# Outer products of a decoder step's sample states as 32-row products, one batch per quadrant of the array

## The chip, the cores and the metric

The kernel runs on one core of one Trainium2 chip. A core has TensorE (matrix products; the profile calls it PE, and its weight loads PEld), VectorE (DVE), ScalarE (ACT), GpSimd (POOL) and SyncE (SP), which issues DMAs. Each engine works through its own queue in order and waits on semaphores for the others. TensorE multiplies a stationary operand (the weights, rows x columns) with a moving one; the rows of both are partitions of the on-chip memory, and the result lands in PSUM. The time is device microseconds of a whole execution; less is better.

## The reference, cut to what matters

One decoder layer for a prompt of 256 tokens and for 8 sample sequences of 8 tokens each, all with d_model 2048 and shared weights: an mLSTM branch (4 heads of 256 x 256 state) and a GLA branch (4 heads of 128 x 256 state) in parallel, merged by gates, then a gated convolutional feed-forward. The samples come with states, one per batch and head, and each is updated with the outer products of that batch's own 8 keys and values:

```python
# mLSTM, per batch b and head h
C_new = decay[..., None, None] * C + jnp.einsum('bhl,blhd,blhe->bhde', w_end, kc, vc)
# GLA, per batch b and head h
S_new = (jnp.exp(b_end)[..., None] * S
         + jnp.einsum('bshd,bshe->bhde', kc * jnp.exp(b_end[:, None] - b), vc))
```

Within a chunk, the outputs also need products of a masked matrix A of token against token (64 x 64 for the samples) with the values. All data is fp32.

## The kernel before, in words

All 320 tokens (256 of the prompt, 64 of the samples) are the moving columns of the weight products. A product with fp32 weights and fp32 activations is made of three products in a faster format with rounded operands (`mm3`, L74 to L76): each operand is split into a rounded part (hi, made by ScalarE, L69 for weights) and the rest (lo, made by VectorE, L70). The results of weight products go to PSUM tiles called `big`, all others to tiles called `mx` (four banks of each kind) and `mxi`.

The stages follow one another: input and norm, then for each head h = 0..3 a GLA head (`gla_head`) and an mLSTM head (`mlstm_head`) with their projections, then the remaining gates, the output projection, and the feed-forward. Which instruction stands where in an engine's queue is decided by a scheduler that simulates the engines when the kernel is built; it interleaves the small work of the heads with the weight products of later projections. In the profiled execution the outer products lie between 146 and 465 us.

The samples' small products use a stack: the 64 sample tokens make two groups g of 32 tokens (4 batches of 8), and a group's 32 tokens stand four times above one another in 128 partitions, in the four quadrants r of 32 rows. In the keys' stack `ks` the quadrants hold hi, lo, hi, lo (`stacked`); in the values' stack `vs` they hold hi, hi, lo, lo (`values`). One product over 128 rows then sums all four combinations of parts, for all four batches of the group at once. To get the outer product of one batch alone, the keys are first multiplied by a mask: `km` holds copies of `ks` in which all rows of other batches are zero (`bm`, one column per batch), and each batch gets its products of 128 rows from `km` and `vs` (L687 in GLA, one per batch; L780 in mLSTM, two per batch). VectorE then adds the result to the decayed state (L691, L783), and a DMA on POOL's queue writes it out.

`sample_values` multiplies A of the samples with the values in the same stacked form: A's two 32 x 32 diagonal blocks are written into the quadrants of `asp` by ScalarE (L494) and VectorE (L496), and two products of 128 rows with `vs` (L498) are added to the result `mxi`, which `inter` began: products of a state with 32 columns of queries per batch, each in its own quadrant of columns (L572).

Further places at which an operand has fewer than 128 rows: transposes of short inputs (64 rows of x, L155; 32 rows of the normaliser state, L317; 64 rows of convolution state, L897) and the spreading of the norm factors (`lh`, L177, fp32, its last product with 64 rows). A product of plain fp32 operands is shown as two passes.

Of the kernel before, what the change touches and what calls it, by code (L numbers as in the profile page):

```python
# [10 lines left out]
F32 = mybir.dt.float32  # L11
# [6 lines left out]
P = 128  # L18
# [25 lines left out]
def step_kernel(ctx: ExitStack, tc: tile.TileContext, a: dict):  # L44
# [190 lines left out]
    with tc.tile_pool(name="mc", bufs=1, reuse_waits="tile") as mc, \  # L235
# [17 lines left out]
        for c0 in (0, 256):  # L253
# [11 lines left out]
        i16 = mc.tile([P, 16], F32, name="i16")  # L265
        nc.gpsimd.memset(i16, 1.0)
        nc.gpsimd.affine_select(i16, i16, pattern=[[-S, 16]], compare_op=ALU.is_ge, fill=0.0, base=0,
                                channel_multiplier=1)
        nc.gpsimd.affine_select(i16, i16, pattern=[[S, 16]], compare_op=ALU.is_ge, fill=0.0, base=S - 1,
                                channel_multiplier=-1)  # L270
        nc.gpsimd.tensor_tensor(i16[:, 0:8], i16[:, 0:8], i16[:, 8:16], op=ALU.add)
        bm = mc.tile([P, 4], F32, name="bm")
        nc.gpsimd.tensor_tensor(bm, i16[:, 0:4], i16[:, 4:8], op=ALU.add)
# [153 lines left out]
        asp = mc.tile([P, 2, P], F32R, name="asp")  # L427
        nc.gpsimd.memset(asp.bitcast(F32), 0.0)

        vH, vL, vs = (mc.tile([P, 2, 264], F32R, name=t)[:, :, 0:258] for t in ("vH", "vL", "vs"))  # L430
        for t, one in ((vH, 1.0), (vL, 0.0), (vs[0:64], 1.0), (vs[64:128], 0.0)):
            nc.gpsimd.memset(t[:, :, 256:258].bitcast(F32), one)

# [17 lines left out]
        def quads(name):  # L451
            t = w320(name)[:, 0:256]
            return t, t.rearrange("p (g r x) -> p g r x", g=2, r=4)

        def tok4(t):

            return t.rearrange("p (g x) -> p g x", g=2).unsqueeze(2).broadcast_to([P, 2, 4, 32])
# [9 lines left out]
        def values(v):  # L467

            pb = mx("mx8")
            for m in range(2):  # L470
                vr, vr4 = quads("vr")
                nc.gpsimd.tensor_copy(vr4, tok4(v[:, m, T:]))
                for g in range(2):
                    nc.tensor.transpose(pb[:, g * 256 + m * P:g * 256 + (m + 1) * P], vr[:, g * P:(g + 1) * P], ident)
            pa = natural(v)
            pav = pa.rearrange("p (j e) -> p j e", j=2)
            nc.scalar.activation(vH[:, :, 0:256], pav, AF.Copy)
            nc.vector.tensor_tensor(vL[:, :, 0:256], pav, vH[:, :, 0:256].bitcast(F32), op=ALU.subtract)
            pbv = pb.rearrange("p (g e) -> p g e", g=2)
            nc.scalar.activation(vs[:, :, 0:256], pbv, AF.Copy)  # L480
            nc.vector.tensor_tensor(vs[64:128, :, 0:256], pbv[64:128], vs[64:128, :, 0:256].bitcast(F32), op=ALU.subtract)
            return vH, vL

        def sample_values(pi, A, w):


            for g in range(2):
                Ag = A[32 * g:32 * g + 32, 32 * g:32 * g + 32].rearrange("p (q t) -> p q t", t=S)

                def quad(r):  # L490
                    return asp[32 * r:32 * r + 32, g].rearrange("p (q y) -> p q y", q=4)[:, :, 8 * g:8 * g + 8]

                for r in (g, g + 2):
                    nc.scalar.activation(quad(r), Ag, AF.Copy)  # L494
                for r in (1 - g, 3 - g):
                    nc.vector.tensor_tensor(quad(r), Ag, quad(g).bitcast(F32), op=ALU.subtract)  # L496
            for g in range(2):
                nc.tensor.matmul(pi[:, 0:w], asp[:, g], vs[:, g, 0:w], start=False, stop=(g == 1))  # L498
# [55 lines left out]
        def stacked(src, w):  # L554
            ks = wk.tile([P, 512], F32R, tag="ks", name="ks", bufs=1)
            nc.scalar.activation(ks[:, 0:w], src, AF.Copy)
            for r in (32, 96):
                nc.vector.tensor_tensor(ks[r:r + 32, 0:w], src[r:r + 32], ks[r:r + 32, 0:w].bitcast(F32), op=ALU.subtract)
            return ks[:, 0:w].bitcast(F32)
# [17 lines left out]
        def gla_head(h, q, k, v):  # L577
# [101 lines left out]
            for b0 in range(0, B, 4):  # L679
                km = wk.tile([P, 512], F32R, tag="km", name="km")  # L680
                kmv = km.rearrange("p (b d) -> p b d", b=4)
                nc.vector.tensor_tensor(kmv, ks[:, 32 * b0:32 * b0 + P].unsqueeze(1).broadcast_to([P, 4, P]),
                                        bm.unsqueeze(2).broadcast_to([P, 4, P]), op=ALU.mult)
                for i in range(0, 4, 2):
                    pS = mx("mx16")
                    for ii in range(2):
                        nc.tensor.matmul(pS[:, ii * 256:(ii + 1) * 256], kmv[:, i + ii], vs[:, b0 // 4, 0:256],  # L687
                                         start=True, stop=True)
                    for ii in range(2):
                        bb = b0 + i + ii  # L690
                        nc.vector.scalar_tensor_tensor(st0[:, bb], st0[:, bb], ebe[:, bb:bb + 1],  # L691
                                                       pS[:, ii * 256:(ii + 1) * 256], op0=ALU.mult, op1=ALU.add)
# [3 lines left out]
        def mlstm_head(h, q, k, v):  # L696
# [40 lines left out]
            for d in range(2):  # L737
                kr, kr4 = quads("kr")
                nc.vector.tensor_tensor(kr4, tok4(k[:, d, T:]), tok4(bc[:, N + 72:N + 136]), op=ALU.mult)
                for g in range(2):  # L740
                    nc.tensor.transpose(pk[:, g * 256 + d * P:g * 256 + (d + 1) * P], kr[:, g * P:(g + 1) * P], ident)
                ksum = wk.tile([P, B], F32, tag="ksum", name="ksum")
                nc.vector.tensor_reduce(ksum.rearrange("p (g b) -> p g b", g=2),
                                        kr4[:, :, 0].rearrange("p g (b t) -> p g b t", t=S),
                                        axis=mybir.AxisListType.X, op=ALU.add)
                nc.vector.tensor_tensor(n1[:, d], n1[:, d], ksum, op=ALU.add)
# [23 lines left out]
            for b0 in range(0, B, 2):  # L770
                km = wk.tile([P, 512], F32R, tag="km", name="km")
                kmv = km.rearrange("p (b d) -> p b d", b=2)
                nc.vector.tensor_tensor(kmv,
                                        ks[:, 256 * (b0 // 4):256 * (b0 // 4) + 256].unsqueeze(1).broadcast_to([P, 2, DH]),
                                        bm[:, b0 % 4:b0 % 4 + 2].unsqueeze(2).broadcast_to([P, 2, DH]), op=ALU.mult)
                for i in range(2):
                    bb = b0 + i
                    pC = mx("mx24")
                    for d in range(2):
                        nc.tensor.matmul(pC[:, d * 256:(d + 1) * 256], kmv[:, i, d * P:(d + 1) * P],  # L780
                                         vs[:, b0 // 4, 0:256], start=True, stop=True)
                    cf = c0t[bb // 4][:, bb % 4, :, 0:DH]
                    nc.vector.scalar_tensor_tensor(cf, cf, dec[:, bb:bb + 1], pC.rearrange("p (c e) -> p c e", c=2),  # L783
# [245 lines left out]
```

## Time and profile before

| what | value |
|---|---|
| time, median of 3 runs | 1915.32 us (1915.15 to 1915.62) |
| the profiled execution's own time | 1914.34 us |
| its span, first to last instruction | 1912.6 us |
| mean granted TensorE clock | 0.996 |
| TensorE products, busy | 1895.9 us (99%), 13123 records |
| VectorE / ScalarE / POOL busy | 1083.9 / 772.8 / 339.3 us |
| outer products in the trace | 32 in GLA (L687), 64 in mLSTM (L780) |

Rows of the profile give line, engine, operation, `out<-in` by the program's names, the weights' rows*columns for a product, the shape, and how many. In a timeline the first number is the start in us from the span's start, the second how long the row lasts from its first start to its last end. The durations of products overlap: each shows some 0.3 us from its start to the end of its results, while the next one starts long before; a product's share of TensorE's time is read from start to start. In tables by stretch, the columns behind the stretch are its length, busy time and count of each engine, the granted clock, the DMA share and GB/s.

### The profile page before, as it was taken

How to read it: one execution, taken by the hardware profiler on the slowest of the kernel's cores; microseconds unless marked ns; L12 is line 12 of the kernel's file. 1: busy time of each engine (PE TensorE's matmuls, PEld its weight loads, DVE VectorE, ACT ScalarE, POOL GpSimd, SP SyncE). 2: the span in 40 equal slices, each digit the busy share in tenths (PEclk: the TensorE clock that was granted, in tenths of full speed). 3: DMA queues.
4: the chain of work that ended last, by engine and by line, in shares of the span. 5: the costliest groups of instructions: out<-in, count | busy, mean ns of one | idle time of the engine just before them, and what ended most of it. 6: DMA issues, size and time to landing. Idle time of an engine off the chain costs nothing.

```text
span 1912.6 us, 32511 instructions
## 1 busy us (share of the span) xinstructions
PE 1895.9 (99%) x13123; PEld 1879.4 (98%) x13123; DVE 1083.9 (57%) x1666; ACT 772.8 (40%) x1096; POOL 339.3 (18%) x614
## 2 busy tenths in 40 slices
PE   9999999999999999999999999999999999999997
PEld 8999999999999999999999999999999999999997
DVE  5768686877544444446555545545554554555455
ACT  5544443454433333333344333433433443343345
POOL 4334241522000000021112102101110210111014
PEclk9999999999999999999999999999999999999998
DMA  8656676756555555565454444444445444444442
GB/s 250 201 140 195 189 220 184 226 171 216 168 146 152 148 150 153 146 189 167 151 151 146 152 153 146 154 146 152 150 148 155 144 154 148 150 153 146 154 148 93
DMA packets 300192, 311.03 MB, mean 163 GB/s; under 512 B 15268, under 2 KB 292026, under 8 KB 300041
## 3 DMA queue, kind: packets, MB, share of 16 engines
q1 hardware_dynamic: 287849, 283.53, 49.0%
q0 software_dynamic: 7296, 23.90, 3.6%
q8 instruction: 103, 1.69, 0.4%
q10 hardware_dynamic: 4896, 1.52, 0.3%
q14 instruction: 48, 0.39, 0.1%
HBM read 286.44 MB, written 22.47 MB: 162 GB/s over the span
## 4 chain that ended last, share of the span: by engine, by line


## 5 line engine op out<-in xcount | busy, mean ns | idle before, releaser
L70 DVE TENSOR_TENSOR wl<-raw,wh 128x1024 fp32r<-128x1024 f32 x504 | 628.6, 1247 | 608.9 <-ACT wh L69 608.4
L69 ACT ACTIVATE wh<-raw 128x1024 fp32r<-128x1024 f32 x504 | 534.4, 1060 | 881.0 <-PE big L75 735.4
L74 PE MATMUL big<-hH,wh 128*128 128x320 f32 x2832 | 878.6, 310 | 0.9 <-ACT wh L69 0.9
L75 PE MATMUL big<-hL,wh 128*128 128x320 f32 x2832 | 879.3, 311 | 0.0
L76 PE MATMUL big<-hH,wl 128*128 128x320 f32 x2832 | 877.5, 310 | 0.0
L74 PEld LDWEIGHTS big<-hH,wh 128*128 128x128 f32 x2832 | 532.3, 188 | 2.6 <-issue 1.2
L75 PEld LDWEIGHTS big<-hL,wh 128*128 128x128 f32 x2832 | 532.4, 188 | 1.0 <-issue 0.4
L76 PEld LDWEIGHTS big<-hH,wl 128*128 128x128 f32 x2832 | 532.3, 188 | 0.6
L75 PE MATMUL big<-aL,wh 128*128 128x320 f32 x704 | 217.9, 310 | 0.0
L76 PE MATMUL big<-aH,wl 128*128 128x320 f32 x704 | 217.6, 309 | 0.0
L74 PE MATMUL big<-aH,wh 128*128 128x320 f32 x704 | 215.8, 309 | 0.0
L76 PEld LDWEIGHTS big<-aH,wl 128*128 128x128 f32 x704 | 132.4, 188 | 0.0
L75 PEld LDWEIGHTS big<-aL,wh 128*128 128x128 f32 x704 | 132.4, 188 | 0.0
L74 PEld LDWEIGHTS big<-aH,wh 128*128 128x128 f32 x704 | 131.8, 188 | 0.0
L924 POOL COPY conv<-u 128x2 f32<-128x2 f32 x44 | 8.3, 188 | 527.4 <-DVE u L921 527.4
L855 POOL TENSOR_TENSOR g<-g 128x320 f32<-128x320 f32 x16 | 14.8, 925 | 366.4 <-DVE g L851 366.4
L75 PE MATMUL big<-mL,wh 128*128 128x320 f32 x256 | 78.8, 309 | 0.0
L74 PE MATMUL big<-mH,wh 128*128 128x320 f32 x256 | 78.7, 309 | 0.0
L76 PE MATMUL big<-mH,wl 128*128 128x320 f32 x256 | 78.7, 309 | 0.0
L962 DVE TENSOR_TENSOR x<-big,x 128x320 f32<-128x320 f32 x96 | 46.6, 488 | 46.5 <-PE big L76 46.5
L936 POOL TENSOR_TENSOR g<-g,uc 128x256 f32<-128x256 f32 x44 | 32.6, 742 | 211.9 <-DVE g L935 211.9
L75 PE MATMUL big<-yL,wh 128*128 128x320 f32 x192 | 59.2, 308 | 0.0
(394 smaller groups left out, 1790.7 us busy)
## 6 DMA issues: line engine op xcount, KB each, us to landing
raw<-in_w_in SPq DMA_DIRECT2D x176, 512.0 KB, 3.9
raw<-in_ffn_w_up SPq DMA_DIRECT2D x88, 512.0 KB, 3.5
raw<-in_ffn_w_gate SPq DMA_DIRECT2D x88, 512.0 KB, 3.7
raw<-in_ffn_w_down SPq DMA_DIRECT2D x88, 512.0 KB, 3.5
raw<-in_w_out SPq DMA_DIRECT2D x32, 512.0 KB, 3.5
C<-in_state_mlstm_C SPq DMA_DIRECT2D x32, 256.0 KB, 5.7
o_C_s<-C POOLq DMA_DIRECT2D x32, 256.0 KB, 4.0
raw<-in_w_branch_a SPq DMA_DIRECT2D x16, 512.0 KB, 3.4
```

Of the source, the lines that this page charges most:

```text
L69: nc.scalar.activation(hi, raw, AF.Copy)
L70: nc.vector.tensor_tensor(lo, raw, hi.bitcast(F32), op=ALU.subtract)
L74: nc.tensor.matmul(out, wh, xh, start=first, stop=False)
L75: nc.tensor.matmul(out, wh, xl, start=False, stop=False)
L76: nc.tensor.matmul(out, wl, xh, start=False, stop=last)
L855: nc.gpsimd.tensor_tensor(sg[m], sg[m], acc[m], op=ALU.add)
L924: nc.gpsimd.tensor_copy(conv1[:, 0:2, c], u[:, T:T + 2])
L936: nc.gpsimd.tensor_tensor(g[:, 0:T], g[:, 0:T], gel[m][:, 0:T], op=ALU.mult)
L962: nc.vector.tensor_tensor(x2[k], pt[:, :N], x2[k], op=ALU.add)
```

## The change

1. The stacks are laid out anew: quadrant r of group g now belongs to one batch, 4g + r, and holds that batch's 8 tokens four times, as the four parts (`quads`, `tok4`). A part's sign is in a table `sel` with a value for each partition, and one helper, `stack`, makes a whole stack in two instructions of 128 rows: ScalarE writes the rounded operand times +1 or -1, VectorE adds the operand times 0 or 1. Before, ScalarE wrote all rows and VectorE subtracted on 64 or twice 32 of them.
2. The outer product of a batch takes the 32 rows of its own quadrant of `ks` and `vs`. The masked copies `km` and the mask `bm` are gone. Each product in GLA has a PSUM bank to itself (`mx16`, half used), and two batches are issued together; in mLSTM, too, two batches have a bank each (`mx24`).
3. `sample_values` needs A's blocks spread over the quadrants in the new layout: two new fp32 products per head (L501) with a constant matrix `put` of 64 rows spread them, and `stack` writes the result into `asp`, twice a head.
4. The set-up of `bm` on POOL is replaced by ten small instructions on VectorE that make `part`, `sel` and `put`.

The PE queue in the first mLSTM head, at the outer products. Names: `km` and `ks` as above, `hH`, `hL` the parts of the activations, `wh`, `wl` those of the weights. Before:

```order
L76 MATMUL big<-hH_105,wl 128x320
L780 MATMUL mx_1811<-vs,km 128x256 x2
L74 MATMUL big<-hH_106,wh 128x320
L75 MATMUL big<-hL_122,wh 128x320
L780 MATMUL mx_1816<-vs,km 128x256 x2
L780 MATMUL mx_1823<-vs,km 128x256 x2
L76 MATMUL big<-hH_106,wl 128x320
L780 MATMUL mx_1828<-vs,km 128x256 x2
```

With the change, the same place. Both products of one PSUM tile (one batch) take the same 32 rows; the next tile takes the next quadrant:

```order
L76 MATMUL big<-hH_118,wl 128x320
L774 MATMUL mx_1810<-vs,ks 128x256 x2
L74 MATMUL big<-hH_115,wh 128x320
L75 MATMUL big<-hL_131,wh 128x320
L774 MATMUL mx_1811<-vs,ks 128x256 x2
L774 MATMUL mx_1820<-vs,ks 128x256 x2
L76 MATMUL big<-hH_115,wl 128x320
L774 MATMUL mx_1821<-vs,ks 128x256 x2
```

The products stand as close to weight products as before; the batches that follow are spread further, with two or three weight products between pairs. In the whole queue the 96 outer products stand in 31 runs between other work before, and in 50 with the change.

The PE queue in the first GLA head, at its outer products. Before, two batches share a tile:

```order
L74 MATMUL big<-hH_112,wh 128x320
L687 MATMUL mx_1206<-vs,km 128x256 x2
L687 MATMUL mx_1211<-vs,km 128x256 x2
L75 MATMUL big<-hL_128,wh 128x320
L687 MATMUL mx_1218<-vs,km 128x256 x2
L76 MATMUL big<-hH_112,wl 128x320
```

With the change; behind these three stand five more, each alone between weight products:

```order
L76 MATMUL big<-hH_113,wl 128x320
L689 MATMUL mx_1207<-vs,ks 128x256
L689 MATMUL mx_1208<-vs,ks 128x256
L689 MATMUL mx_1213<-vs,ks 128x256
L74 MATMUL big<-hH_114,wh 128x320
L75 MATMUL big<-hL_130,wh 128x320
```

The eight products of a GLA head stood in three runs, and now stand in six.

The PE queue where the first GLA head's new spreading products stand, with the numerator products (L518) behind them; the sample product L505 that needs their result comes after another 16 weight products:

```order
L76 MATMUL big<-hH_104,wl 128x320
L501 MATMUL mx_1123<-AT,put 128x32 x2
L518 MATMUL mx_1136<-vH,AH 128x256
L518 MATMUL mx_1136<-vL,AH 128x256
L518 MATMUL mx_1136<-vH,AL 128x256
```

L501 is new work in the queue; before, A went to `asp` by ScalarE and VectorE alone.

The diff, cut to its core:

```diff
-        i16 = mc.tile([P, 16], F32, name="i16")
...
-        bm = mc.tile([P, 4], F32, name="bm")
-        nc.gpsimd.tensor_tensor(bm, i16[:, 0:4], i16[:, 4:8], op=ALU.add)
+        part = mc.tile([P, 4], F32, name="part")
+        sel = mc.tile([P, 5], F32, name="sel")
...
+        put = mc.tile([64, 2, P], F32, name="put")
+        nc.vector.tensor_copy(put.rearrange("p g (q r t) -> p (g q) r t", q=4, r=4),
+                              ident[0:64, 0:64].rearrange("p (b t) -> p b t", t=S).unsqueeze(2).broadcast_to([64, B, 4, S]))
...
+        def stack(dst, src, c):
+            nc.scalar.activation(dst, src, AF.Copy, scale=sel[:, c:c + 1])
+            nc.vector.scalar_tensor_tensor(dst, src, sel[:, c + 1:c + 2], dst.bitcast(F32), op0=ALU.mult, op1=ALU.add)
...
-            nc.scalar.activation(vs[:, :, 0:256], pbv, AF.Copy)
-            nc.vector.tensor_tensor(vs[64:128, :, 0:256], pbv[64:128], vs[64:128, :, 0:256].bitcast(F32), op=ALU.subtract)
+            stack(vs[:, :, 0:256], pbv, 2)
...
         def sample_values(pi, A, w):
+            pe = mx("mx30")
             for g in range(2):
-                Ag = A[32 * g:32 * g + 32, 32 * g:32 * g + 32].rearrange("p (q t) -> p q t", t=S)
...
+                nc.tensor.matmul(pe[:, 32 * g:32 * g + 32], put[:, g], A[:, 32 * g:32 * g + 32], start=True, stop=True)
             for g in range(2):
-                nc.tensor.matmul(pi[:, 0:w], asp[:, g], vs[:, g, 0:w], start=False, stop=(g == 1))
+                stack(aspv[:, g], pe[:, 32 * g:32 * g + 32].rearrange("p (q t) -> p q t", q=4), 0)
+            for g in range(2):
+                nc.tensor.matmul(pi[:, 0:w], asp[:, g * P:(g + 1) * P], vs[:, g, 0:w], start=False, stop=(g == 1))
...
         def stacked(src, w):
             ks = wk.tile([P, 512], F32R, tag="ks", name="ks", bufs=1)
-            nc.scalar.activation(ks[:, 0:w], src, AF.Copy)
-            for r in (32, 96):
-                nc.vector.tensor_tensor(ks[r:r + 32, 0:w], src[r:r + 32], ks[r:r + 32, 0:w].bitcast(F32), op=ALU.subtract)
-            return ks[:, 0:w].bitcast(F32)
+            stack(ks[:, 0:w], src, 0)
+            return ks
...
-            for b0 in range(0, B, 4):
-                km = wk.tile([P, 512], F32R, tag="km", name="km")
...
-                    for ii in range(2):
-                        nc.tensor.matmul(pS[:, ii * 256:(ii + 1) * 256], kmv[:, i + ii], vs[:, b0 // 4, 0:256],
-                                         start=True, stop=True)
...
+            for b0 in range(0, B, 2):
+                pS = [mx("mx16"), mx("mx16")]
+                for i in range(2):
+                    g, r = b0 // 4, slice(32 * ((b0 + i) % 4), 32 * ((b0 + i) % 4) + 32)
+                    nc.tensor.matmul(pS[i][:, 0:256], ks[r, g * P:(g + 1) * P], vs[r, g, 0:256], start=True, stop=True)
...
             for b0 in range(0, B, 2):
-                km = wk.tile([P, 512], F32R, tag="km", name="km")
...
+                pC = [mx("mx24"), mx("mx24")]
+                for d in range(2):
+                    for i in range(2):
+                        g, r = b0 // 4, slice(32 * ((b0 + i) % 4), 32 * ((b0 + i) % 4) + 32)
+                        nc.tensor.matmul(pC[i][:, d * 256:(d + 1) * 256], ks[r, g * 256 + d * P:g * 256 + (d + 1) * P],
+                                         vs[r, g, 0:256], start=True, stop=True)
```

More of the change, by code (lines that the diff above doesn't have):

```diff
@@ L424, in step_kernel @@
         nT = mc.tile([P, 2, 36], F32, name="nT")
-        asp = mc.tile([P, 2, P], F32R, name="asp")
+        asp = mc.tile([P, 272], F32R, name="asp")
         nc.gpsimd.memset(asp.bitcast(F32), 0.0)
+        aspv = asp.rearrange("p (g x) -> p g x", x=136)[:, :, 0:128].rearrange("p g (q y) -> p g q y", y=32)[:, :, :, 0:S]
         vH, vL, vs = (mc.tile([P, 2, 264], F32R, name=t)[:, :, 0:258] for t in ("vH", "vL", "vs"))
-        for t, one in ((vH, 1.0), (vL, 0.0), (vs[0:64], 1.0), (vs[64:128], 0.0)):
+        for t, one in ((vH, 1.0), (vL, 0.0)):
             nc.gpsimd.memset(t[:, :, 256:258].bitcast(F32), one)
+        nc.vector.tensor_copy(vs[:, :, 256:258], sel[:, 4:5].unsqueeze(2).broadcast_to([P, 2, 2]))
         def proj2(tag, c0, scale):
@@ L770, in mlstm_head @@
             for b0 in range(0, B, 2):
[L771 to L775 removed]
+                pC = [mx("mx24"), mx("mx24")]
+                for d in range(2):
+                    for i in range(2):
+                        g, r = b0 // 4, slice(32 * ((b0 + i) % 4), 32 * ((b0 + i) % 4) + 32)
+                        nc.tensor.matmul(pC[i][:, d * 256:(d + 1) * 256], ks[r, g * 256 + d * P:g * 256 + (d + 1) * P],
+                                         vs[r, g, 0:256], start=True, stop=True)
                 for i in range(2):
                     bb = b0 + i
[L778 to L781, printed above, removed]
                     cf = c0t[bb // 4][:, bb % 4, :, 0:DH]
[L783 removed]
+                    nc.vector.scalar_tensor_tensor(cf, cf, dec[:, bb:bb + 1], pC[i].rearrange("p (c e) -> p c e", c=2),
                                                    op0=ALU.mult, op1=ALU.add)
```

41 lines of the change are left out of this document (15 added, 26 removed).

## The prediction

> **What bounds the kernel now.** I read the page first, then TensorE's waits, then busy time by stretch. The chain of work that ended last came back empty for this run, so it can't be used.
>
> ```profile
> span 1912.6 us, 32511 instructions
> PE 1895.9 (99%) x13123; PEld 1879.4 (98%) x13123; DVE 1083.9 (57%) x1666; ACT 772.8 (40%) x1096; POOL 339.3 (18%) x614
> ```
> ```profile
> engine line waited for: us in total, times, longest us
> PE mx L632 <- POOL lv_z L624: 1.8, 2, 1.3
> PE mx L112 <- DVE ones L98: 1.1, 1, 1.1
> PE big L74 <- ACT wh L69: 0.9, 1, 0.9
> ```
> ```profile
> core 0: us, PE busy (x) PEld busy (x) DVE busy (x) ACT busy (x) POOL busy (x), PEclk, DMA share, GB/s
> 98.00:102.00 4.00, 2.47 (x17) 1.95 (x15) 4.00 (x10) 1.96 (x4) 3.99 (x5) 1.00 0.70 71
> 103.00:106.50 3.50, 3.50 (x16) 3.50 (x15) 3.50 (x11) 1.21 (x2) 3.12 (x5) 0.51 0.36 125
> 107.00:480.00 373.00, 373.00 (x2773) 364.12 (x2772) 280.88 (x585) 171.18 (x331) 114.18 (x163) 1.00 0.64 195
> 480.00:1900.00 1420.00, 1420.00 (x9694) 1418.79 (x9693) 725.40 (x926) 538.88 (x664) 175.18 (x337) 1.00 0.49 150
> ```
>
> TensorE is busy 99% of the span and waits under 5 us in all. From 107 to 480 us, where all the outer products lie, it has no gap, while VectorE works 281 of 373 us and ScalarE 171. Weight products stand between all the small ones, so TensorE never runs dry. The time is therefore the sum of TensorE's intervals: whatever an edit adds to or takes from its queue lands on the end, and what it saves on VectorE is worth nothing beyond those few microseconds of waits.
>
> **What an outer product costs now, and what a narrow one costs.** The first rows group the old products; behind them stands the timeline of TensorE's products, then weight loads, at places where an operand has fewer rows or columns than 128 (start, duration, rows*columns of the weights).
>
> ```profile
> L780 PE MATMUL mx<-vs,km 128*128 128x256 f32 x64 | 10.7, 279 | 0.0
> L687 PE MATMUL mx<-vs,km 128*128 128x256 f32 x32 | 5.5, 280 | 0.0
> 178.42 0.40 PE L780 MATMUL mx<-vs,km 128*128 128x256 f32 x2
> 178.66 0.31 PE L74 MATMUL big<-hH,wh 128*128 128x320 f32 x1
> ```
> ```profile
> 978.72 0.31 PE L76 MATMUL big<-hH,wl 128*128 128x320 f32 x1
> 978.96 0.27 PE L897 MATMUL mx<-ident,cr 64*128 64x64 f32 x1
> 979.16 0.41 PE L74 MATMUL big<-hH,wh 128*128 128x320 f32 x1
> 979.41 0.30 PE L75 MATMUL big<-hL,wh 128*128 128x320 f32 x1
> ```
> ```profile
> 63.42 0.31 PE L74 MATMUL big<-hH,wh 128*128 128x320 f32 x1
> 63.66 0.30 PE L317 MATMUL mx<-ident,n0r 32*128 32x32 f32 x2
> 63.90 0.42 PE L75 MATMUL big<-hL,wh 128*128 128x320 f32 x1
> ```
> ```profile
> 63.66 0.19 PEld L317 LDWEIGHTS mx<-ident,n0r 32*128 32x128 f32 x2 [0.19 <-PE big L75]
> 63.89 0.19 PEld L75 LDWEIGHTS big<-hL,wh 128*128 128x128 f32 x1
> 64.00 0.19 PEld L76 LDWEIGHTS big<-hH,wl 128*128 128x128 f32 x1
> ```
> ```profile
> 37.93 0.43 PE L177 MATMUL mx<-ident,lh 64*128 64x64 f32 x2
> 38.29 0.41 PE L75 MATMUL big<-hL,wh 128*128 128x320 f32 x1
> ```
> ```profile
> 113.96 1.07 PE L572 MATMUL mxi<-S,qz 128*32 128x256 f32 x16
> 114.63 0.40 PE L572 MATMUL mxi<-S,qz 128*32 128x256 f32 x4
> 114.96 0.41 PE L75 MATMUL big<-hL,wh 128*128 128x320 f32 x1
> ```
>
> Durations of products overlap, so I read starts. Weight products start every 0.147 us (1420 us hold 9694 products after 480 us). Two old outer products take 178.42 to 178.66, 0.24, so one costs about 0.117: its 256 columns, with its weight load hidden behind the product before it. All 96 of them: 96 x 0.117 = 11.2 us.
>
> At every place where the rows in use change to 32 or 64 of 128, the neighbours are no longer hidden:
> - Entering: 978.72 to 978.96 and 63.42 to 63.66, 0.24 instead of 0.147, so 0.093 more.
> - Leaving: the first weight product starts together with its own load (63.89 and 63.90), and the next one comes 0.25 later (979.16 to 979.41), 0.103 more than 0.147. Two loads in a row start 0.11 apart (63.89, 64.00): I take 0.107 for a load of 128 columns.
> - The stay itself, from first narrow start to first weight product: 0.20 for one 64-column transpose (978.96 to 979.16), 0.36 for one fp32 product of 64 rows in its two passes (37.93 to 38.29). The last burst of the 32-column products stays 0.31 after its last start (four starts within 0.02, so 114.65, to 114.96). Its four bursts start (114.63 - 113.96)/3 = 0.22 apart, which is what 256 fp32 columns take; the rest, some 0.09, is the array running empty, the 0.093 of entering over again. I take 0.095.
>
> The Trainium skill, "TensorEngine Tiling (Array Packing)", Key Properties, states that changing the tiling mode, not just the tile, drains TensorE; by that rule the 32-row products pay what these narrow transposes pay. The trace agrees in its 0.24 at 63.66.
>
> **The change, part by part.**
>
> *Outer products (old L687, L780; new L689, L774).* Still 96 of 256 columns, now with 32 rows. The issue order of the change has them in 50 separate runs between full-height work: 20 single products and 4 runs of three in the GLA heads; 20 pairs, 4 runs of two pairs and 2 runs of four alternating in the mLSTM heads. Each run is entered and left. A single: enter 0.093; stay load 0.107 + 256 columns 0.107 + empty 0.095 = 0.309; leave 0.103; together 0.505 us. Bounds: the stay of the transpose (0.20) gives 0.396; a stay at the fp32 burst's 0.31 plus a load of 0.107 gives 0.61. I take 0.505, because the 0.36 of L177 comes out the same way (two loads 0.214, 64 fp32 columns a quarter of 0.22, empty 0.095).
> The other 46 products lie inside runs. In 30 the one before is in the same quadrant: I take 0.107, the load hidden behind the running product, because L317's two loads on the same 32 rows fit into 0.19 (bounds 0.107 and, load not hidden, 0.214). In 16 the quadrant is another: L572's four column quadrants start within 0.02, so 0.007 (upper bound 0.117, one after the other).
> Sum 50 x 0.505 + 30 x 0.107 + 16 x 0.007 = 28.6 us, less the old 11.2: **+17.3 us**. Bounds: 50 x 0.396 + 3.2 + 0.1 - 11.2 = +11.9, and 50 x 0.61 + 6.4 + 1.9 - 11.2 = +27.6.
>
> *The spreading products (new L501).* Once in each of 8 heads, two fp32 products with 64 rows, each in two passes, are issued that were not there. 64 rows is a switch again: enter 0.093, four loads 0.428, 32 fp32 columns 0.027, empty 0.095, leave 0.103: 0.745 each, **+6.0 us**. Bounds: 0.396 x 8 = 3.2 as the transpose, and 6.8 with a tenth more each.
>
> *The 32-column products (L572, now L577)* come in 9 runs instead of 8, one being split: 0.093 + 0.095 + 0.103, **+0.3 us**.
>
> *VectorE, ScalarE, POOL.*
>
> ```profile
> L70 DVE TENSOR_TENSOR wl<-raw,wh 128x1024 fp32r<-128x1024 f32 x504 | 628.6, 1247 | 608.9 <-ACT wh L69 608.4
> L69 ACT ACTIVATE wh<-raw 128x1024 fp32r<-128x1024 f32 x504 | 534.4, 1060 | 881.0 <-PE big L75 735.4
> L773 DVE TENSOR_TENSOR km<-ks,bm 128x512 fp32r<-128x512 f32 x16 | 13.3, 854 | 0.0
> L682 DVE TENSOR_TENSOR km<-ks,bm 128x512 fp32r<-128x512 f32 x8 | 5.2, 688 | 0.1
> L558 DVE TENSOR_TENSOR ks<-mx,ks 32x512 fp32r<-32x512 f32 x8 | 5.5, 690 | 0.2
> L783 DVE SCALAR_TENSOR_TENSOR C<-C,dec,mx 128x512 f32<-128x512 f32 x32 | 22.9, 738 | 3.0 <-PE mx L780 3.0
> L496 DVE TENSOR_TENSOR asp<-AT,asp 32x32 fp32r<-32x32 f32 x16 | 2.9, 182 | 1.6 <-ACT asp L494 1.2
> L494 ACT ACTIVATE asp<-AT 32x32 fp32r<-32x32 f32 x16 | 3.7, 229 | 9.2 <-DVE AT L643 8.9
> ```
>
> VectorE loses the 24 masked copies (18.5 us) and half the splits of the keys; a split of a whole tile in one instruction costs about L783's 0.74. It saves some 22 us of 281, all under TensorE's cover: worth 0 us. Its ten set-up instructions for the part signs and the spreading matrix stand before the long 85-to-107 us stretch, where VectorE still had idle time; POOL's old mask set-up goes, also under cover: 0. GLA outputs take eight half-used banks instead of four full ones, each freed by one update as before; the order puts weight products between them: 0.
> The new chain in each head is spreading product, ScalarE, VectorE, ScalarE, VectorE, then the sample product L505. With one weight split ahead on each engine (L69, L70) it takes 1.06 + 2 x 0.23 + 1.25 + 2 x 0.18 = 3.1 us. Between L501 and L505 stand 25 rows or more, in the first head 9 numerator products and 16 weight products: 9 x 0.117 + 16 x 0.147 = 3.4 us. The cover is thin, so I take 0 and keep up to 0.4 us x 8 = 3 for the range; behind L505 all of TensorE queues.
>
> **Sum:** 17.3 + 6.0 + 0.3 = +23.6 us on the profiled execution's own 1914.34 (span 1912.6 and 1.7 around it): 1937.9. The median of runs is 1.0 higher, 1915.32, which gives 1938.9; I say **1938**. Bounds +15.4 and +37.7 (27.6 + 6.8 + 0.3 + 3).
>
> **Rivals.**
> 1. *No drain for products of this kind (not slower).* The rows above are transposes and fp32 products; the 64-column products L754, of the same type as the new ones, disturb nothing:
>
> ```profile
> 157.83 0.34 PE L753 MATMUL mx<-qL,kH 128*128 128x256 f32 x1
> 158.18 0.34 PE L753 MATMUL mx<-qH,kL 128*128 128x256 f32 x1
> ```
>
> One of them lies in each such round of three, and the round takes 0.35, three loads. If 32-row products kept the pace, 80 of them would cost 0.117 and 16, on another quadrant than the one before, 0.007: 9.5, so -1.7; the spreading products still add four loads each, 3.4 in all: +1.7, so 1917, no change. Were all 96 to overlap in fours as L572's columns do, 24 x (0.117 + 3 x 0.007) = 3.3 would stand for 11.2, and with the spreading products the kernel would be 4.5 us faster, 1911. The price decides: with less than (3.8 - 1.7)/58 = 0.04 us for each of the 58 switches, instead of the 0.39 that a single costs over 0.117, the kernel is within 0.2%. Against it stand all four narrow places above; and of four quadrants at most three ever stand together, mostly one. The Trainium skill, "TensorE: Matmul & The Clock Gate", Part 3, gives 3.07 times the speed for four 32-row tiles side by side; by it the 11.2 us would be an estimated 3.6. No run here shows it.
> 2. *The clock gate closes.* After TensorE worked 2.47 of 4 us (98 to 102 us) the granted clock fell to about half for 3.4 us. If runs every two or three weight products look as idle as that, each head may lose one such window, 1.7 us: eight to twelve of them, +14 to +20, 1952 to 1958. Against: a run with two weight products behind it lasts some 0.9 us, of which 0.4 without a product streaming (twice empty, twice a load); the 98-102 stretch idles 0.4 of its time too, but in one piece of 1.3; and the 16 narrow products at 114 us close nothing.
> 3. *Earlier relief.* The waits at 98 to 107 us and the half clock behind them (1.8 + 1.7 us) vanish because POOL and VectorE have less set-up: -3.5, 1934.5 with the rest. Against: both engines are full there with work that stays.
>
> **From these to numbers.** My case 0.82; no drain 0.08 (0.05 at 1917, 0.03 with overlap in fours); clock gate 0.06; relief 0.04. Within 0.2% (3.8 us, about what a measurement of this kernel can tell from no change) falls only the no-drain case. Slower 0.92, same 0.05, faster 0.03. The range leaves out the no-drain case and most of the clock case; inside mine it reaches from near the lower bound, 1929, to 1950, most of the way to the upper.
>
> **What would show it.** Right: in the profile after, the weight product behind each L774 or L689 run starts with its load and is followed 0.25 us later by the next; a single L689 takes about 0.31 from its start to the next weight product; VectorE's busy time falls by 20 us or so without effect; TensorE's records stay near 13,100 and the span grows by about 24. Wrong: weight products behind the runs at 0.147; or a stretch of 0.5 in the clock row inside a head; or waits of L505 for asp.

## Result and profile after

| | before | after |
|---|---|---|
| time, median (lowest to highest) | 1915.47 us (1915.15 to 1916.17, 4 runs) | 1946.35 us (1944.06 to 1948.07, 4 runs) |
| the profiled execution's own time | 1914.34 us | 1944.06 us |

The changed kernel is slower: the ratio is 1.0163, 95% interval 1.0151 to 1.0175. That is 30.9 us by the medians and 29.7 us by the two profiled executions. The prediction was 1938, range 1929 to 1950, so it has the sign and the range right and is 8 us short.

The head of the page after:

```profile
span 1942.3 us, 32488 instructions
PE 1923.6 (99%) x13155; PEld 1887.6 (97%) x13155; DVE 1061.3 (55%) x1628; ACT 775.5 (40%) x1084; POOL 336.1 (17%) x607
```

VectorE works 22.6 us less (1083.9 before), and the kernel is longer by more than that: VectorE was not the bound. TensorE has 32 records more, the spreading products, and is still busy for 99% of a longer span, because the records' durations overlap at the costly places too: the weight product behind a run lasts 0.41 to 0.43 us instead of 0.31. The loss is therefore not in the busy column; it is between starts. The timeline of TensorE's products after shows a run of three outer products, a single one, and runs of two and of four (start, duration, rows*columns):

```profile
149.09 0.39 PE L689 MATMUL mx<-vs,ks 32*128 32x256 f32 x3
149.40 0.43 PE L74 MATMUL big<-hH,wh 128*128 128x320 f32 x1
...
151.72 0.31 PE L74 MATMUL big<-hH,wh 128*128 128x320 f32 x1
151.96 0.38 PE L689 MATMUL mx<-vs,ks 32*128 32x256 f32 x1
152.27 0.42 PE L75 MATMUL big<-hL,wh 128*128 128x320 f32 x1
152.52 0.31 PE L76 MATMUL big<-hH,wl 128*128 128x320 f32 x1
```
```profile
192.32 0.31 PE L76 MATMUL big<-hH,wl 128*128 128x320 f32 x1
192.56 0.50 PE L774 MATMUL mx<-vs,ks 32*128 32x256 f32 x2
192.99 0.41 PE L74 MATMUL big<-hH,wh 128*128 128x320 f32 x1
193.24 0.31 PE L75 MATMUL big<-hL,wh 128*128 128x320 f32 x1
193.49 0.50 PE L774 MATMUL mx<-vs,ks 32*128 32x256 f32 x4
193.92 0.41 PE L76 MATMUL big<-hH,wl 128*128 128x320 f32 x1
```

The single one is entered in 151.96 - 151.72 = 0.24, stays 0.31 to the next weight product, and the one behind that comes 0.25 later: 0.505 in all over a queue without it (0.093 + 0.309 + 0.103), as in the working. The three at 149.09 stay 0.31 as well, since they lie in three quadrants and start together. A pair in one quadrant stays 192.56 to 192.99 = 0.43, and four products over two quadrants (193.49 to 193.92) stay no longer.

The spreading product, on the same engine:

```profile
123.42 0.31 PE L76 MATMUL big<-hH,wl 128*128 128x320 f32 x1
123.66 0.63 PE L501 MATMUL mx<-AT,put 64*128 64x32 f32 x4
124.22 0.38 PE L518 MATMUL mx<-vH,AH 128*128 128x256 f32 x1
```

It enters in 0.24 and stays 0.56, against 0.55 in the working.

TensorE's waits after hold something that the table of before did not have, in the second GLA head. The waits come first (us in all, times, longest), then the timeline of TensorE's products, then rows from the one of VectorE, then busy time by stretch:

```profile
PE mx L672 <- DVE kd L665: 2.7, 1, 2.7
PE mx L637 <- POOL lv_z L629: 1.6, 1, 1.6
```
```profile
240.06 0.82 PE L548 MATMUL mx<-ident,hs 128*128 128x128 f32 x6
243.59 0.33 PE L672 MATMUL mx<-ident,kd 128*128 128x128 f32 x1 [2.72 <-DVE kd L665]
244.13 0.33 PE L673 MATMUL mx<-ident,kr 128*128 128x128 f32 x1 [0.21 <-DVE kr L667]
245.20 0.41 PE L74 MATMUL big<-hH,wh 128*128 128x320 f32 x1 [0.52 <-DVE gk L131]
```
```profile
239.02 0.48 DVE L544 TENSOR_SCALAR hs<-mxi,sc 128x256 f32<-128x256 f32 x1 [1.01 <-POOL sc L536]
240.70 0.48 DVE L550 TENSOR_SCALAR hn<-mx,vecT 128x256 f32<-128x256 f32 x1 [1.20 <-PE mx L548]
241.88 0.41 DVE L661 TENSOR_TENSOR kd<-gb 128x256 f32<-128x256 f32 x1
242.96 0.58 DVE L665 TENSOR_TENSOR kd<-kd,gk 128x256 f32<-128x256 f32 x1 [0.54 <-ACT kd L664]
```
```profile
245.50:249.00 3.50, 3.50 (x15) 3.50 (x14) 0.92 (x3) 1.18 (x2) 0.00 (x0) 0.51 0.00 0
```

`kd` is the keys scaled by their decay, and `kr`, made from it, the samples' part laid out for the stack; the state updates of that head are made from these two. VectorE has it in its queue behind the norm of the head's outputs: the norm's factors come from POOL (239.02), then the norm needs the transposes L548 from TensorE (240.70), and only then does VectorE begin `kd` (241.88), by way of ScalarE (L664). TensorE has nothing between the last L548 and L672, waits 2.72, waits twice more, and the clock granted in the 3.5 us behind that is 0.51: 12 weight products there start 0.12 later than they would. In the issue order, TensorE's queue between these two steps reads as follows, before (row number, line, operation):

```
1353 L541 MATMUL mx9_2167<-ident_67,hs_2155 128x128 x2
1354 L74 MATMUL big_2987<-hH10_113,wh_3051 128x320
...
1410 L76 MATMUL big_3362<-hH4_107,wl_3397 128x320
1411 L667 MATMUL mx14_2184<-ident_67,kd_2175 128x128
```

and after:

```
1438 L548 MATMUL mx9_2159<-ident_67,hs_2147 128x128 x2
1439 L672 MATMUL mx14_2176<-ident_67,kd_2167 128x128
```

The 57 weight products that covered the chain in the queue before stand elsewhere after. In the two traces all four GLA heads have 57 at this place before; after they have 57, none, 42 and 57. The trace of before has these steps at 222 and 231 us, 9 us apart, without a wait:

```profile
222.21 0.81 PE L541 MATMUL mx<-ident,hs 128*128 128x128 f32 x6
231.22 0.27 PE L667 MATMUL mx<-ident,kd 128*128 128x128 f32 x1
```

### The profile page after: what moved, and what is told of

It is laid out like the page before. It is cut to its first block, busy times and chain, and to the rows that moved or that the text cites. A ratio compares the mean times of both kernels' runs of the same rounds, so it can differ in the third digit from the quotient of the medians.

```text
span 1942.3 us, 32488 instructions
## 1 busy us (share of the span) xinstructions
PE 1923.6 (99%) x13155; PEld 1887.6 (97%) x13155; DVE 1061.3 (55%) x1628; ACT 775.5 (40%) x1084; POOL 336.1 (17%) x607
## 4 chain that ended last, share of the span: by engine, by line
```

## Experiments

Theory: each entry into and exit from 32- or 64-row work costs TensorE about 0.2 us and the stay some 0.3 or more, for outer products and spreading products alike, and the late `kd` costs the rest. Rivals: the price is one of the new layout or of another engine and not of the number of rows; the loss is a matter of the clock; the wait for `kd` only stands where TensorE would have waited anyway.

The times hold something that no change here made. The first transpose of the normaliser state (`n0r`, L317 before) starts between 63.5 and 67.1 us in the thirteen traces, before any outer product; and from the first transpose of convolution state (`cr`, L897 before) to the end all of them take 946.4 to 946.6 us. Between these two rows lie all the heads. That stretch, in one execution each, tells the kernels apart better than the times do; where 3.4 us of it run at half clock, that costs some 1.5 us (13 starts, each 0.12 late).

| kernel | `n0r` to `cr`, us | of it at half clock, us |
|---|---|---|
| before | 902.5 | 3.4 (at 103, behind waits for `lv_z`) |
| after | 930.8 | 3.4 (at 245.5, behind the wait for `kd`) |
| after, outer products on 128 rows | 915.4 | 6.8 (behind the wait for `kd`) |
| the same, and the spreading products too | 913.0 | 3.4 (behind the wait for `kd`) |
| before, on 32 / 64 / 96 rows | 913.0 / 913.1 / 900.4 | none |
| after, scaled keys early | 927.1 | none |
| after, eight products in a closed section | 951.3 | 27.3 |
| the same, spreading products on 128 rows and early keys | 937.3 | 23.9 |
| after, fewer runs without a section | 920.4 | none |
| the same, spreading products on 128 rows and early keys | 919.0 | 3.4 (at 190.8) |
| after, both kinds of product on 128 rows, early keys | 906.9 | none |

### The outer products on 128 rows

The queue and all other work stay; only the operands are cut differently, so each product sums the four batches of its group.

```diff
-  ks[r, g * P:(g + 1) * P], vs[r, g, 0:256]
+  ks[:, g * P:(g + 1) * P], vs[:, g, 0:256]
-  ks[r, g * 256 + d * P:...], vs[r, g, 0:256]
+  ks[:, g * 256 + d * P:...], vs[:, g, 0:256]
```

> The changed kernel, with the outer products on all 128 rows instead of 32 (each sums four batches, so the sample states differ); issue order, stacks and spreading products as they are. Theory (entering and leaving 32 rows empties TensorE): 50 runs lose 0.196 us of entering and leaving, and the products go from 18.6 to 11.2 us: 17.2 us less than the changed kernel, 1929 us. Rival (the loss lies in waits for VectorE or ScalarE, or in the banks, not in the rows): no change, 1946 us.

Measured: 1930.06 us (1929.14 to 1930.58), 1.0079 of before (1.0064 to 1.0094). 16.3 us are gone against the changed kernel by the row count alone. The wait for `kd` is still there with the same 2.7 us. The stretch of the heads is 15.4 us shorter, although the half clock behind that wait lasts twice as long in this profile; start to start, the outer products and the steps into and out of their runs take 17.1 us less.

### The spreading products on 128 rows as well

`put` is padded with zero rows to 128, and 128 rows of A are read.

```diff
-  put = mc.tile([64, 2, P], F32, name="put")
+  put = mc.tile([P, 2, P], F32, name="put")
+  nc.vector.memset(put, 0.0)
-  sample_values(pi, ATs, 256)
+  sample_values(pi, AT[:, 384:448], 256)
```

> As before it, and the spreading products too on 128 rows, with zeros in the added rows. Theory: each of the 8 spreading runs drops from 0.745 us to four loads, 0.45: another 2.4 us less, 1927 us, which leaves 3.6 us of spreading and the wait at 240 us with its half clock, some 5 us, over the kernel before. Rival (the spreading costs by its rows nothing): as the run on full rows alone.

Measured: 1925.87 us (1924.51 to 1927.04), 1.0057 (1.0042 to 1.0072), another 4.2 us where 2.4 were expected. The products are still there, with two passes each; they only cease to switch: a head's four passes are entered in 0.15 instead of 0.24, stay 0.36 instead of 0.56 and are left in 0.20 instead of 0.22, which is 2.5 us for eight heads, and the stretch of the heads is 2.4 us shorter. The rest of the 4.2 is not shown to come from the switch: of the 5.0 us between the two profiled executions, 2.7 lie ahead of the first head.

### The kernel before, with fewer rows

The other direction, on the old kernel with its old layout and its masked copies: its outer products read only the first 32, 64 or 96 rows of `km` and `vs`. That leaves out the products of the lower parts that lie in the other quadrants (hi times hi remains with 32 rows), nothing else; in the expectation below "only some batches' terms" is a slip of mine, since all batches keep their own.

```diff
-  nc.tensor.matmul(pS[...], kmv[:, i + ii], vs[:, b0 // 4, 0:256], ...)
+  nc.tensor.matmul(pS[...], kmv[0:32, i + ii], vs[0:32, b0 // 4, 0:256], ...)
```

> The kernel before, with its outer products on the first 32 of the 128 rows (only some batches' terms are summed, so the sample states differ); masked copies, stacks and order as they are. Theory: 31 runs at 0.505 us, and 65 further products at 0.12 on the same quadrant, 23.5 us for the old 11.2: 12.3 us more, 1928 us. Rival (32 rows cost nothing by themselves): 1915.5 us.

> The kernel before, with its outer products on the first 64 rows (sample states differ). Theory (any change of the row group in use empties the array): as with 32 rows, weight products behind each run at 0.25 us, 1928 us. Rival (only 32-row products do): 1915.5 us.

> The kernel before, with its outer products on the first 96 of the 128 rows (the terms of the last quadrant are left out). Theory (only a row group of 32 or 64, not any shorter operand, empties the array): 1915 us, weight products behind the runs at 0.147 us. Rival (any change of the rows in use does): 1928 us as with 32 and 64.

Measured: 32 rows 1927.74 us (1924.69 to 1928.88), 1.0069 (1.0052 to 1.0086); 64 rows 1927.49 and 96 rows 1914.84 in one execution each. In the stretch of the heads, where neither the start nor a half clock disturbs these three, 32 and 64 rows take 12.6 and 12.7 us more than 96 (1.2 of it because the 96-row profile waits less ahead of the outer products), where 12.3 were expected. One place in TensorE's timeline in each, first with 32 rows:

```profile
177.70 0.31 PE L76 MATMUL big<-hH,wl 128*128 128x320 f32 x1
177.94 0.49 PE L780 MATMUL mx<-vs,km 32*128 32x256 f32 x2
178.37 0.42 PE L74 MATMUL big<-hH,wh 128*128 128x320 f32 x1
178.62 0.31 PE L75 MATMUL big<-hL,wh 128*128 128x320 f32 x1
```

with 64 rows:

```profile
180.44 0.31 PE L76 MATMUL big<-hH,wl 128*128 128x320 f32 x1
180.68 0.49 PE L780 MATMUL mx<-vs,km 64*128 64x256 f32 x2
181.11 0.41 PE L74 MATMUL big<-hH,wh 128*128 128x320 f32 x1
```

and with 96 rows:

```profile
178.53 0.31 PE L76 MATMUL big<-hH,wl 128*128 128x320 f32 x1
178.68 0.40 PE L780 MATMUL mx<-vs,km 96*128 96x256 f32 x2
178.92 0.31 PE L74 MATMUL big<-hH,wh 128*128 128x320 f32 x1
```

The pair with 32 or 64 rows is entered in 0.24 and stays 0.43; with 96 rows it is entered in 0.15 and stays 0.24, as with 128. The price needs neither the new layout nor the new instructions on VectorE, and it is not one of leaving rows unused: it falls between 64 and 96 rows. The Trainium skill, "TensorEngine Tiling (Array Packing)", Key Properties, says that a change of the tiling mode drains the engine. The three timelines agree with it if 64 rows count as another mode and 96 rows as the mode of the full array.

### The scaled keys early

In `gla_head` the block that makes `kd` and `kr` is written ahead of the sample products and the norm.

```diff
   bs = b[:, T:].rearrange("p (b t) -> p b t", t=S)
+  kd = w320("kd")
+  ... (the block that fills kd and kr, unchanged)
   qe = wk.tile([P, 1, 64], F32, tag="qe", name="qe", bufs=1)
   ...
   normed(list(numerators("mx13", AT, vn, 256)) + [pi], ...)
-  kd = w320("kd")
-  ...
```

> The changed kernel, with the decayed keys kd and kr of a GLA head computed ahead of the sample products and the head norm in the program, so that VectorE's queue holds them ahead of the norm's steps. Theory (in the second GLA head TensorE waits 2.7 us for kd, 0.9 around it, and 3.4 us of half clock follow, 1.5): these 5 us go, 1941 us. Rival (the wait only moves to the norm's own steps, or another head): 1946 us.

Measured: 1940.43 us (1939.95 to 1942.12), 1.0138 (1.0121 to 1.0155): 5.9 us less than the changed kernel, and 3.8 less in the stretch of the heads. TensorE's waits there have no `kd` any more, and the half-clock stretch at 245 us is gone with it; of the rival, 1.0 us came true, as a new wait for masks of A (`AT`):

```profile
PE mx L637 <- POOL lv_z L629: 1.6, 1, 1.6
PE big L74 <- ACT wh L69: 1.2, 1, 1.2
PE mx L112 <- DVE ones L98: 1.1, 1, 1.1
PE mx L637 <- DVE AT L640: 1.0, 2, 0.6
```

### Eight products in a closed section

If runs are what costs, few long runs should cost little. The eight products of a head or group take four banks, one for each quadrant, and stand in a section into which the scheduler puts nothing else.

```diff
+  pS = [mx("mx16") for _ in range(4)]
+  with tc.tile_critical():
+      for g in range(2):
+          for i in range(4):
+              r = slice(32 * i, 32 * i + 32)
+              nc.tensor.matmul(pS[i][:, g * 256:(g + 1) * 256], ks[r, g * P:(g + 1) * P], vs[r, g, 0:256], ...)
```

> The changed kernel, with the outer products in 12 closed runs of eight, one after the other on four quadrants and four banks (GLA: all eight batches; mLSTM: four batches at a time). Theory: a run costs entering 0.093, load 0.107, two waves of 0.12, three quadrants more 0.02, emptying 0.095, leaving 0.103: 0.66 each, 7.9 us, instead of the 28.4 measured in the change (18.6 in the products and 9.8 of entering and leaving): 20.5 us less, 1926 us. Rival 1 (four quadrants take turns): 0.505 + 7 x 0.117 = 1.32 a run, 15.9 us, 1934 us. Rival 2 (holding four banks at once makes TensorE wait for the updates): above 1940 us.

> The closed runs of eight, the spreading products on 128 rows, and kd ahead of the norm, all three together. Theory: 1926 less 2.4 less 5, 1918 to 1919 us, that is, the kernel before within some 3 us. Rival (the three terms don't add, since waits take over): above 1926 us.

Measured: 1966.02 us (1965.66 to 1967.09), 1.0273 (1.0258 to 1.0288), and with the spreading products on 128 rows and the early keys besides 1948.32 (1946.99 to 1951.83), 1.0183 (1.0167 to 1.0198). Both theory values (1926, 1918 to 1919) are missed by far. The first kernel's timeline at two of its twelve sections, and its busy time by stretch behind the first of them:

```profile
151.88 0.31 PE L75 MATMUL big<-hL,wh 128*128 128x320 f32 x1
153.99 0.74 PE L690 MATMUL mx<-vs,ks 32*128 32x256 f32 x8 [1.80 <-DMA bc<-rows]
154.82 0.63 PE L76 MATMUL big<-hH,wl 128*128 128x320 f32 x1
...
196.41 0.51 PE L778 MATMUL mx<-vs,ks 32*128 32x256 f32 x8 [1.30 <-ACT lv_d L627]
197.01 0.41 PE L74 MATMUL big<-hH,wh 128*128 128x320 f32 x1
```
```profile
154.80:157.40 2.60, 2.58 (x10) 2.59 (x11) 2.39 (x7) 0.53 (x1) 0.00 (x0) 0.50 0.08 28
```

The products themselves stay less than on 128 rows, though longer than in the theory: eight stay 196.41 to 197.01 = 0.60, where the theory has 0.46 without entering and leaving (0.107 + 2 x 0.12 + 0.02 + 0.095) and 128 rows would cost 8 x 0.117 = 0.94. Why they stay longer in a section is open. And TensorE stands still ahead of the sections, by the profile for work that their products do not read (`bc` from a DMA at 153.99): ten gaps of 1.6 to 4.5 us from weight product to section, some 26 us in all, and eight half-clock stretches between 155 and 553 us (one of them behind `kd`), in which 81 products start 0.12 late, 10 us. 26 + 10 covers most of the 40 us by which it missed 1926. That four banks are held at once (rival 2) is not the reason: the next experiment holds them too, without a section, and has none of these gaps. The experiment priced the closed section and left the number of runs untested as a cause of the total.

### Fewer runs without a closed section

The same grouping, with the first product issued on the bank that is claimed last and the other seven right behind it; the scheduler stays free. Then the same with the two other repairs, and the two repairs with the outer products on 128 rows.

```diff
+  with tc.high_priority():
+      lead = prod(0, 3)
+      with tc.issue_after(lead.ins):
+          for g, i in ((0, 0), (0, 1), (0, 2), (1, 3), (1, 0), (1, 1), (1, 2)):
+              prod(g, i)
```

> Everything as in the changed kernel, but the four banks of a group are all claimed first and its eight outer products queue right behind the first of them: 33 separate runs instead of 58 in the trace (50 in the issue order of the changed kernel), none of them closed off from other work. Theory (each run pays for entering, running empty and leaving, and a further quadrant 0.007): four runs of six 0.64, twenty pairs 0.61, nine mixed ones of four 0.63 to 0.73, some 21 us for all outer products instead of 28.5: 1938 to 1939. Rival (the price hangs on the number of products with 32 rows, not on the number of runs): 96 products as before, 1946.

> The same grouping (35 runs here), with the spreading products on 128 rows and the scaled keys of the GLA heads ahead of the sample product. If the three costs add up: 1946.35 less 6.9 for the grouping, less 4.2 for the spreading products (the step from the outer products on 128 rows to both on 128), less 5.9 for the early keys: 1929. Rival (the early keys and the grouping take the same wait away, or the earlier products make a new one): 1934 or more.

> Both kinds of product on 128 rows (the outer products then sum four batches) and the scaled keys early: no drain and no late keys are left, so what remains above the kernel before is the work of the spreading products, 16 of them in two passes, some 3.6 us with their loads, and 1 to 2 of further waits: 1920 to 1921. Rival (the half-clock stretch behind the late keys is not their doing): 1925 to 1926.

(The 58 in the first text counts the eight runs of spreading products too, in which nothing changes here; like for like it is 33 against 50, and the sum there was made with 50.)

Measured: 1934.83 us (1934.45 to 1937.17), 1.0109 (1.0093 to 1.0126); 1932.74 (1931.05 to 1934.37), 1.0094 (1.0079 to 1.0109); 1921.68 (1918.38 to 1922.83), 1.0034 (1.0022 to 1.0046).

Grouping took 11.5 us where 8 were expected, with the same 96 products of 32 rows: the price hangs on runs and not on products. Start to start, the outer products and what their entering and leaving adds take 20.4 us instead of 28.1, so the grouping itself gave 7.7, as expected. The surplus is mostly the wait for `kd`. In this kernel's queue 14 weight products stand between the two steps, and its timeline there has

```profile
240.14 0.31 PE L76 MATMUL big<-hH,wl 128*128 128x320 f32 x1
241.11 0.33 PE L672 MATMUL mx<-ident,kd 128*128 128x128 f32 x1 [0.66 <-DVE kd L665]
```

0.66 instead of 2.72, and no half clock behind it. So part of what the early keys gave was already taken, the 4.2 put down for the spreading products was 2.4 by the rows, and with all three repairs the sum came to 1932.7 instead of 1929, between the two expectations. The only run of eight in this kernel, which no section closes, stays 0.45, as the theory of the closed runs had it:

```profile
435.95 0.52 PE L691 MATMUL mx<-vs,ks 32*128 32x256 f32 x8
436.40 0.41 PE L74 MATMUL big<-hH,wh 128*128 128x320 f32 x1
```

That kernel shows one more thing, in the first mLSTM head: four pairs in a row with two or three weight products between, without any wait of TensorE, and behind them a stretch at half clock (timeline, then busy time by stretch):

```profile
187.41 0.50 PE L783 MATMUL mx<-vs,ks 32*128 32x256 f32 x2
...
190.48 0.57 PE L783 MATMUL mx<-vs,ks 32*128 32x256 f32 x2
190.98 0.64 PE L74 MATMUL big<-hH,wh 128*128 128x320 f32 x1
```
```profile
187.00:191.00 4.00, 4.00 (x21) 2.61 (x19) 4.00 (x7) 1.30 (x2) 2.18 (x5) 0.97 0.86 250
190.90:194.00 3.10, 3.10 (x12) 3.02 (x12) 3.10 (x6) 0.90 (x2) 2.77 (x2) 0.50 0.92 278
```

That the pairs closed the clock is not shown: the changed kernel has four pairs almost as close together (198.39, 199.46, 200.53 and 201.59 us), and its clock stays full behind them.

The third kernel, without the switches of these products and without the wait, came to 1921.7 against 1920 to 1921: the largest part of what then stands above the kernel before is the spreading products, whose four passes a head take 2.9 us from start to start over all of them; then come short waits for masks of A (1.0 us in its table of waits, none before). About 2 us of its 6.9 are not attributed. No version beats the kernel before; of those that do the whole work the best is the grouped one with both repairs, 0.9% slower.

## Why the prediction was right, point by point

- **Bound.** "What an edit adds to TensorE's queue lands on the end, and what it saves on VectorE is worth nothing": 22.6 us less on VectorE, 30.9 us longer.
- **Outer products, +17.3.** The run on 128 rows puts them at 16.3 by the medians and at 17.1 by the rows of the two traces. Entering 0.24, a single's stay 0.31 and leaving 0.25 are the values of the working. A pair stays 0.43, not 0.416. The quadrants overlap, as taken from the four column quadrants: four products in two quadrants stay as long as two in one, and so do six that start three and three in the grouped kernel (0.43); eight that start four and four stay 0.45. The stay goes by how many products follow each other in one quadrant.
- **Spreading products, +6.0.** 8 x (0.56 + 0.093 + 0.103) = 6.05 from the rows after. On 128 rows 2.5 of it come back by the rows, because the passes themselves remain.
- **The split run of 32-column products, +0.3.** Start to start, all these products take 12.08 us after and 11.52 before: 0.56, and the ninth run is entered and left besides.
- **Cover of the new chain, taken at 0 with 0.4 us a head kept for the range.** No wait of L505 occurs, so the 0 was right there.
- **The step that failed** is the 0 for VectorE, ScalarE and POOL "under cover". The working looked for lost cover at the new chain only. The scheduler had built the whole queue anew, and the second GLA head's `kd` had lost the 57 weight products that covered it. That term was 0. It needed no chip to be suspected: the issue order shows the consumer L672 directly behind L548, and the trace of before has 9 us between these two steps. Its size reads in the rows after: the six L548 start 0.11 apart from 240.06, so the last at 240.6, and from there to the weight product at 245.20 pass 4.6 us for work of some 0.6; with 1.4 us of half clock behind it (12 x 0.12) that is 5.4. The early keys took away 5.9 by the medians, and 3.8 in the stretch of the heads, where the new wait of 1.0 for masks of A came in.
- **The sum.** With 5.4 it is 23.6 + 5.4 = 29.0. The stretch of the heads grew by 28.3, although before holds a half clock of some 1.5 us at 103 us that the profile after does not have there; without that one the growth is 29.8. The other 1.4 of the 29.7 between the profiled executions lie ahead of the first head (`n0r` at 63.66 and 65.08) and are not shown to be the change's.
- **Luck.** That 1946 lies inside the range owes something to luck. The room up to 1950 was kept for dearer products and for the cover of the new chain; both came as in the sum, and a term that was not in the working filled the room.
- **Rivals.** *No drain* falls with the rows after and, without the new layout, with 64 against 96 rows. The Trainium skill's 3.07 times for four tiles ("TensorE: Matmul & The Clock Gate", Part 3) is a figure for the tiles side by side. Here eight products in four quadrants stay 0.45 instead of 0.94, 2.1 times; with 0.2 for entering and leaving such a run saves 0.29 us (0.14 in a closed section, where it stays 0.60), and a single loses 0.39. *The clock gate closes*: its sign, a stretch of 0.5 inside a head, did appear, but behind the wait for `kd`, and it is gone with that wait. Only in the grouped kernel with both repairs does one stand behind runs, for 3.4 us, and there the cause is open. *Earlier relief*: a wait of 1.6 us for `lv_z` stays, of 1.8. The half clock behind it is not in the profile after; but it is not in those of the kernel before with 32 and 64 rows either, which wait 1.8 us there as before, so its absence is not shown to be the change's doing.

## What to carry to other kernels

Count the places at which TensorE changes between full-height work and work on 64 or fewer rows, not the products: each costs about 0.2 us around it and a stay of 0.31, or 0.43 to 0.45 where two products follow each other in one quadrant. So a single narrow product between weight products costs four times what the full-height one with zeros in it costs (0.505 and 0.117 us), and of the runs seen here only those of six and of eight products came out ahead (0.63 and 0.65 us against 0.70 and 0.94). When a scheduler rebuilds the queue, compare the distance in rows of every producer and consumer pair around the change, not only of the new ones. Don't buy long runs with a closed section: here ten of the twelve held TensorE up for 1.6 to 4.5 us.

## What was not expected of the hardware

- 64 rows are as dear as 32 (1927.49 and 1927.74 us), 96 rows as cheap as 128 (1914.84).
- TensorE's granted clock falls to half behind less idle time than I had thought: behind a gap of 2.1 us from start to start (151.88 to 153.99), and once behind four narrow pairs in 3.6 us with no wait at all. The Trainium skill, "TensorE: Matmul & The Clock Gate", Part 1, HAM oscillation, gives the rule to leave no idle gaps above about 3.4 us. In these two places no gap was that long and the clock fell. It does not always fall: behind the same waits of 1.8 us at about 100 us it did in the profile of before (clock 0.51) and did not in those with 32 and 64 rows (1.00).
- Narrow products in different quadrants run at the same time: one and three, each in a quadrant of its own, stay 0.31 us; two, four and six, with two in each quadrant, 0.43; eight 0.45.
